# One-hot tiles in pairs of tokens, and a longer first part of the expert layer, in a hybrid decoder layer

## The chip, the cores and the metric

The kernel runs on one core of one Trainium2 chip. The metric is the device time of one execution in microseconds (us); of several executions the median is taken. A profile is one execution recorded by the hardware profiler; its span is the time from its first to its last recorded instruction. The engines are TensorE (PE for its matmuls, PEld for its weight loads), VectorE (DVE), ScalarE (ACT), GpSimd (POOL) and SyncE (SP), which issues most DMAs.

## The reference

One decoder layer over 256 tokens of width 1024: a convolution branch and a sparse attention branch, a cross attention over 256 memory rows, and then a mixer that chooses among 16,384 experts. The change lies in that mixer alone:

```python
q = (hn @ w_q).reshape(B, T, PEER_HEADS, 2, PEER_HALF)
s = jnp.einsum('bthpd,hpkd->bthpk', q, sub_keys).astype(jnp.float32)
s_top, i_top = lax.top_k(s, PEER_TOPK)
cand = s_top[..., 0, :, None] + s_top[..., 1, None, :]
cand_idx = i_top[..., 0, :, None] * PEER_KEYS + i_top[..., 1, None, :]
best, pos = lax.top_k(cand.reshape(B, T, PEER_HEADS, n_cand), PEER_TOPK)
experts = jnp.take_along_axis(cand_idx.reshape(B, T, PEER_HEADS, n_cand), pos, axis=-1)
gates = jax.nn.softmax(best, axis=-1)
...
a = jax.nn.gelu(jnp.einsum('nd,nkd->nk', xc, u))
return jnp.einsum('nk,nkd->nd', gc * a, v_emb[ec])
```

Each token has 8 heads with 16 experts each. An expert's number is a pair (i1, i2) of two numbers below 128.

## The kernel before

**The expert mixer as dense products.** The kernel gathers no expert rows. It computes gelu(u . x) for all 16,384 experts and all tokens, multiplies by a matrix of gates that is zero where an expert was not chosen, and multiplies the result with all rows of v. The experts come in 128 chunks of 128 (KEYS = 128). Chunk i holds, with i2 fixed to i, the 128 values of i1 on the partitions, and a tile of 256 tokens beside them.

**A chunk of u (`u_chunk`, L989).** One DMA on SP brings 512 KB (`raw`, four buffers). `wsplit` makes of each half a rounded part `hi` on ACT (L137) and a remainder `lo` (L138) on an engine that the call names: GpSimd (G) for chunks below J = 36, VectorE (V) for the others. `proj` then runs 24 matmuls of 256 columns (L148 to L150: hi x hn_h, hi x hn_l, lo x hn_h for eight slices of the width). A gelu on ACT empties the PSUM tile `pu`.

**The choice.** Meanwhile VectorE finds for each half (hf) of the tokens the top 16 of each of the 16 score rows, builds the sums, takes their top 16 (L901 to L926), subtracts the best (`ge`, L928), and works out the chosen pairs (L931 to L953) as two tables `ix`. `choice_gates` (L959) then takes the exponential of `ge` on ACT (L962), sums and divides on VectorE (L964 to L967). `picked_out` (L970) turns i1, i2 and the gate of a half by a transpose on PE and stores them as f16 tiles i1T, i2T, gTh and gTl (128 choices on the partitions, 256 tokens).

**The first part (loop at L994).** For chunks 0 to J-1 the gelu (L999) goes to `slA`. `choice_gates` is written before chunk J-12 = 24, the six calls of `picked_out` before chunks J-6 to J-1.

**The second part (`while`, L1025).** Chunks J to 127 go on, and the gate matrix is built four tokens at a time in 64 blocks (`gates4`, L1004), spread evenly over chunks. A block makes four one-hot tiles of 128 x 4 numbers on VectorE: o1 (128 choices against the 128 values of i1, L1011), o2 (against i2, L1012), and o2 times the two parts of the gate, oh and ol (L1013, L1014). The token is the innermost of a tile's two axes. For each of the four tokens two matmuls of 128 columns follow (L1016 with oh, L1017 with ol), with o1[:, :, j] as weights and oh[:, :, j] as moving operand, so 128 x 128 gates per token in the PSUM tile `pw`. VectorE multiplies the part of `pw` whose chunks are done into slA and slB (L1021); ACT copies the rest into slB (L1022), where the gelu of a later chunk is multiplied in (L1030, L1034).

**The value part (loop at L1074).** For each chunk, 12 matmuls of 512 columns add the gated activations times v into four PSUM tiles Y (L1070). `gfin`, the gain of the final norm, is written in the text with value chunk 122 (L1081) and takes the place of `hn_l`, which the last chunk of u reads.

**The order of the work.** PE runs in the order of the text. The instructions of the other engines are ordered when the program is built, by a planner with its own estimates of durations; each engine then runs its queue strictly in that order. Buffers of one tag (o0 to o3, `hi`, `lo`, `raw`, `pw`) are reused in turn, and an instruction that overwrites one waits for its readers.

Of the kernel before, what the change touches and what calls it, by code (L numbers as in the profile page):

```python
# [12 lines left out]
F16 = mybir.dt.float16  # L13
# [3 lines left out]
ALU = mybir.AluOpType  # L17
# [3 lines left out]
P = 128  # L21
# [71 lines left out]
def build(tc, A, out, dbg=None):  # L93
    nc = tc.nc
    V, S, G, PE = nc.vector, nc.scalar, nc.gpsimd, nc.tensor
# [13 lines left out]
    def C(name):  # L109
        a, b = CC[name]  # L110
        return con1[:, a:b] if b <= NCON1 else con2[:, a - NCON1:b - NCON1]
# [8 lines left out]
    def wload(src, n=1024):  # L120
        cnt[0] += 1
        raw = wts.tile([P, 1024], F32, name=f"raw{cnt[0]}", tag="raw", bufs=4)
        if cnt[0] == 1:
            nc.sync.dma_start(raw[:, 0:512], src[:, 0:512])
            nc.sync.dma_start(raw[:, 512:], src[:, 512:])
        else:
            nc.sync.dma_start(raw[:, 0:n], src)
        return raw, cnt[0]

    def wsplit(w, engs=None, width=P, half=512):  # L130
        raw, i = w
        out_ = []
        for q in range(2):
            hi = wts.tile([P, 512], F32R, name=f"hi{i}{q}", tag="hi", bufs=6)[:, 0:half]
            lo = wts.tile([P, 512], F32R, name=f"lo{i}{q}", tag="lo", bufs=6)[:, 0:half]
            r = raw[:, half * q:half * q + half]
            S.activation(hi, r, AF.Copy)  # L137
            (engs or (V, V))[q].tensor_sub(lo, r, hi.bitcast(F32))  # L138
            for j in range(half // width):
                out_.append((hi[:, j * width:(j + 1) * width], lo[:, j * width:(j + 1) * width]))  # L140
        return out_

    def wchunk(src, engs=None, width=P):

        return wsplit(wload(src), engs, width)

    def mm3(ps, w, xh, xl, start, stop):
        PE.matmul(ps, w[0], xh, start=start, stop=False)  # L148
        PE.matmul(ps, w[0], xl, start=False, stop=False)  # L149
        PE.matmul(ps, w[1], xh, start=False, stop=stop)  # L150

    def proj(ps, w, x, ks=range(KC)):
        for k in ks:
            mm3(ps, w[k], x[0][:, k], x[1][:, k], k == 0, k == KC - 1)
# [7 lines left out]
    i1T, i2T, gTh, gTl = [tk.tile([P, T], F16, name=n) for n in ("i1T", "i2T", "gTh", "gTl")]  # L162
# [12 lines left out]
    def psum(w, name, tag="mm"):  # L175
        return pm.tile([P, 512], F32, name=name, tag=tag, bufs=4)[:, :w]
# [82 lines left out]
    u = ch.tile([P, 4, 30 + T], F32, name="u")  # L259
# [84 lines left out]
    for i in range(2):  # L344
        G.memset(KV[i], 0.0)
        ps = psum(T, f"pkv{i}")
# [44 lines left out]
    for i in range(6):  # L391
        dst = kraw[i] if i < 2 else qraw[:, i - 2]
        ps = psum(T, f"pq{i}")
# [83 lines left out]
    for i in range(2):  # L477
# [3 lines left out]
        for jj in range(16):  # L481
            PE.matmul(phv, w1[i][:, jj], KV[i][:, :, 2 * jj:2 * jj + 16 * (NC_CMP - 1) + 1:16],
                      start=(jj == 0), stop=(jj == 15))
# [216 lines left out]
    for i in range(2, KC):  # L700
        ps = psum(T, f"pwo{i}")
# [118 lines left out]
    for i in range(2, KC):  # L820
        ps = psum(T, f"pmw{i}")
# [27 lines left out]
    for i in range(16):  # L849
        ps = psum(T, f"ppq{i}")  # L850
# [16 lines left out]
    hn_h = h2p.tile([P, KC, T], F32R, name="hn_h", tag="act_h")  # L867
    hn_l = h2p.tile([P, KC, T], F32R, name="hn_l", tag="act_l")
# [13 lines left out]
    for nh, c in ((0, 0), (1, 0), (1, 1), (0, 1)):  # L882
        PE.matmul(Y[nh][c], zero[:, 0:P], zero, start=True, stop=False, skip_group_check=True)
        for k in range(4):
            PE.matmul(Y[nh][c][:, k * P:(k + 1) * P], h2T[:, 4 * c + k, nh * P:(nh + 1) * P], C("ident"),
                      start=False, stop=False, skip_group_check=True)
# [9 lines left out]
    for hf in range(2):  # L896
# [36 lines left out]
        for side in range(2):  # L933
# [12 lines left out]
            oh = tp.tile([P, 16, P], F16, name=f"ohx{hf}{side}", tag="ohx")  # L946
# [12 lines left out]
    def choice_gates():  # L959
        for hf in range(2):  # L960
            ge = picked[hf][2]
            S.activation(ge, ge, AF.Exp)  # L962
            gs = tp.tile([P, 8], F32, name=f"gs{hf}", tag="gs")
            V.tensor_reduce(gs, ge, axis=AX.X, op=ALU.add)  # L964
            V.reciprocal(gs, gs)
            gt = picked[hf][2] = tp.tile([P, P], F32, name=f"gt{hf}", tag=f"gt{hf}")
            V.tensor_tensor(gt.rearrange("p (k h) -> p h k", h=8), ge, gs.unsqueeze(2).to_broadcast([P, 8, 16]), op=ALU.mult)  # L967
            show(f"g_{hf}", gt)

    def picked_out(hf, j):  # L970

        sl = slice(hf * P, hf * P + P)
        pt = pp.tile([P, 512], F32, name=f"ptk{hf}{j}", tag="w", bufs=2)[:, 0:P]
        PE.transpose(pt, picked[hf][j], C("ident"))
        if j < 2:
            S.activation((i1T, i2T)[j][:, sl], pt, AF.Copy)
        else:
            S.activation(gTh[:, sl], pt, AF.Copy, scale=GSC)
            V.scalar_tensor_tensor(gTl[:, sl], pt, GSC, gTh[:, sl], op0=ALU.mult, op1=ALU.subtract)


    J = 36
    e1 = outer.enter_context(tc.tile_pool(name="e1", bufs=1, side="left", **RW))
    slA = e1.tile([P, J, T], F32, name="slA")
    tmp = outer.enter_context(tc.tile_pool(name="tmp", bufs=2, side="left", **RW))
    iota4 = tmp.tile([P, P, 4], F16, name="iota4", bufs=1)
    V.tensor_copy(iota4, C("iota").unsqueeze(2).to_broadcast([P, P, 4]))

    def u_chunk(i):  # L989
        ps = pp.tile([P, 512], F32, name=f"pu{i}", tag="w" if i < J - 8 and i % 4 > 1 else "s", bufs=2)[:, 0:T]  # L990
        proj(ps, wchunk(A["u"][i], (G, G) if i < J else (V, V)), (hn_h, hn_l))
        return ps

    for i in range(J):  # L994
        if i == J - 12:
            choice_gates()
        if i >= J - 6:
            picked_out((i - J + 6) // 3, (i - J) % 3)
        S.activation(slA[:, i], u_chunk(i), AF.Gelu_apprx_tanh)  # L999
# [3 lines left out]

    def gates4(n0, done):  # L1004
        pw = pp.tile([P, 512], F32, name=f"pw{n0}", tag="w", bufs=2).rearrange("p (n i) -> p n i", n=4)
        o1, o2, oh, ol = [tmp.tile([P, P, 4], F16, name=f"o{t}{n0}", tag=f"o{t}", bufs=1 if t == 1 else 2) for t in range(4)]

        def over_i(t):
            return t[:, n0:n0 + 4].unsqueeze(1).to_broadcast([P, P, 4])

        V.tensor_tensor(o1, iota4, over_i(i1T), op=ALU.is_equal)  # L1011
        V.tensor_tensor(o2, iota4, over_i(i2T), op=ALU.is_equal)  # L1012
        V.tensor_tensor(oh, o2, over_i(gTh), op=ALU.mult)  # L1013
        V.tensor_tensor(ol, o2, over_i(gTl), op=ALU.mult)  # L1014
        for j in range(4):
            PE.matmul(pw[:, j], o1[:, :, j], oh[:, :, j], start=True, stop=False)  # L1016
            PE.matmul(pw[:, j], o1[:, :, j], ol[:, :, j], start=False, stop=True)  # L1017
        for sl_, x0, x1 in ((slA, 0, J), (slB, J, done)):
            if x1 > x0:
                va = sl_[:, 0:x1 - x0, n0:n0 + 4].rearrange("p i n -> p n i")  # L1020
                V.scalar_tensor_tensor(va, pw[:, :, x0:x1], 1.0 / GSC, va, op0=ALU.mult, op1=ALU.mult)  # L1021
        S.activation(slB[:, done - J:, n0:n0 + 4].rearrange("p i n -> p n i"), pw[:, :, done:], AF.Copy, scale=1.0 / GSC)  # L1022

    i, ng = J, 0
    while i < KEYS or ng < T:  # L1025
        if i < KEYS:
            ps = u_chunk(i)
            if ng:
                tt = tmp.tile([P, T], F32, name=f"ua{i}", tag="ua", bufs=3)
                S.activation(tt[:, 0:ng], ps[:, 0:ng], AF.Gelu_apprx_tanh)  # L1030
            if ng < T:
                S.activation(slB[:, i - J, ng:], ps[:, ng:], AF.Gelu_apprx_tanh)
            if ng:
                V.tensor_mul(slB[:, i - J, 0:ng], slB[:, i - J, 0:ng], tt[:, 0:ng])  # L1034
            i += 1
        while ng < min(T, (i - J) * T // (KEYS - 3 - J)):
            gates4(ng, i)
            ng += 4
# [35 lines left out]
    for i in range(KEYS):  # L1074
        a = slA[:, i] if i < J else slB[:, i - J]
# [94 lines left out]
```

## Time and profile before

| | |
|---|---|
| median of 3 runs (lowest, highest) | 1144.11 us (1143.82, 1146.87) |
| the profiled execution, its own time | 1143.92 us |
| its span | 1142.1 us |
| mean granted TensorE clock, share of full | 0.984 |
| PE busy / PEld busy | 1095.2 us (96%) / 1005.4 us (88%) |
| DVE busy / ACT busy / POOL busy | 884.2 us (77%) / 591.8 us (52%) / 111.2 us (10%) |

Busy time is the union of an engine's recorded instructions. An instruction's duration overlaps the next one's on the same engine, so what an instruction costs in a row of others is the distance from its start to the next start. Matmuls overlap most; their ends are modelled, their starts are recorded. In the timeline a row gives start, duration, engine, line, operation, tile written <- tiles read, and in brackets the idle time ahead of it and what ended it.

The mixer's stages in the span: the first part up to about 463 us, the second up to about 785 us, the value part to the end.

### The profile page before, as it was taken

What the parts mean: (1) busy time and instruction counts of PE and PEld (TensorE: products, weight loads), DVE (VectorE), ACT (ScalarE), POOL (GpSimd) and SP (SyncE); (2) the same over time, 40 slices, a digit from 0 to 9 for tenths busy, and PEclk for the clock granted to TensorE, in tenths of its full rate; (3) what the DMA queues carried; (4) which work ended last, traced back from release to release, by engine and by line L of the source; (5) the groups of instructions that cost most, each with busy time, mean ns of one, the idle gap of its engine ahead of it and who ended that gap; (6) DMA issues with size and microseconds to landing.
All of it is one profiled execution on the core that took longest, in us unless ns stands there. A gap on an engine that the chain in (4) does not pass through costs nothing.

```text
span 1142.1 us, 20622 instructions
## 1 busy us (share of the span) xinstructions
PE 1095.2 (96%) x7361; PEld 1005.4 (88%) x7362; DVE 884.2 (77%) x2229; ACT 591.8 (52%) x1354; POOL 111.2 (10%) x86
## 2 busy tenths in 40 slices
PE   8889999999999489999999999999999999999997
PEld 7878778999999489999999999999888888888885
DVE  7998847888889994778888889996666666666665
ACT  5731456665455155555555554445555555555554
POOL 0000000000068389000000000000000000000000
PEclk9899999999999889999999999999999999999999
DMA  8542224625434235544444454446555566565662
GB/s 277 194 127 94 74 99 152 197 90 185 154 124 149 93 114 200 167 156 141 150 147 160 137 161 137 151 144 203 191 196 193 194 192 195 192 196 191 196 192 86
DMA packets 51688, 182.47 MB, mean 160 GB/s; under 512 B 5761, under 2 KB 6529, under 8 KB 51457
## 3 DMA queue, kind: packets, MB, share of 16 engines
q1 hardware_dynamic: 51296, 180.62, 48.2%
q8 instruction: 58, 0.95, 0.3%
q10 hardware_dynamic: 288, 0.52, 0.1%
q14 instruction: 46, 0.37, 0.1%
HBM read 179.81 MB, written 1.05 MB: 158 GB/s over the span
## 4 chain that ended last, share of the span: by engine, by line
PE 87%; DVE 4%; issue 3%; POOL 2%; DMA 1%; ACT 1%; SPq 0%; POOLq 0%; ACTq 0%; DVEq 0%
PE Y L1070 30%; PE pu L150 10%; PE pu L149 10%; PE pu L148 10%; PE pw L1016 3%; PE pw L1017 3%; PE pmk L442 3%; POOL lo L138 2%; PE pmv L458 2%; PE ppq L148 1%; PE ppq L149 1%; PE ppq L150 1%; DVE lo L138 1%; PE pmw L149 1%; PE pmw L148 1%
## 5 line engine op out<-in xcount | busy, mean ns | idle before, releaser
L137 ACT ACTIVATE hi<-raw 128x512 fp32r<-128x512 f32 x632 | 380.6, 624 | 198.7 <-PE pu L149 78.0
L138 DVE TENSOR_TENSOR lo<-raw,hi 128x512 fp32r<-128x512 f32 (+1 forms) x560 | 371.1, 685 | 32.8 <-ACT hi L137 26.4
L148 PE MATMUL pu<-hn_h,hi 128*128 128x256 f32 x1024 | 296.9, 290 | 18.3 <-ACT hi L137 18.3
L150 PE MATMUL pu<-hn_h,lo 128*128 128x256 f32 x1024 | 291.6, 285 | 2.5 <-POOL lo L138 2.5
L149 PE MATMUL pu<-hn_l,hi 128*128 128x256 f32 x1024 | 290.8, 284 | 0.0
L148 PEld LDWEIGHTS pu<-hn_h,hi 128*128 128x128 f32 x1024 | 198.0, 193 | 18.7 <-ACT hi L137 18.5
L150 PEld LDWEIGHTS pu<-hn_h,lo 128*128 128x128 f32 x1024 | 196.7, 192 | 4.6 <-POOL lo L138 4.5
L149 PEld LDWEIGHTS pu<-hn_l,hi 128*128 128x128 f32 x1024 | 197.2, 193 | 0.0
L1070 PE MATMUL Y<-hi,ah 128*128 128x512 f32 x512 | 158.2, 389 | 0.0
L1070 PE MATMUL Y<-lo,ah 128*128 128x512 f32 x512 | 158.1, 389 | 0.0
L1070 PE MATMUL Y<-hi,al 128*128 128x512 f32 x512 | 158.1, 389 | 0.0
L1070 PEld LDWEIGHTS Y<-lo,ah 128*128 128x128 f32 x512 | 96.1, 188 | 20.0
L1070 PEld LDWEIGHTS Y<-hi,al 128*128 128x128 f32 x512 | 96.1, 188 | 19.8
L1070 PEld LDWEIGHTS Y<-hi,ah 128*128 128x128 f32 x512 | 96.1, 188 | 19.9
L158 DVE TENSOR_TENSOR al<-slB,ah 128x256 fp32r<-128x256 f32 x92 | 39.1, 425 | 89.9 <-PE Y L1070 89.9
L138 POOL TENSOR_TENSOR lo<-raw,hi 128x512 fp32r<-128x512 f32 x72 | 103.7, 1473 | 36.6 <-ACT hi L137 36.3
L157 ACT ACTIVATE ah<-slB 128x256 fp32r<-128x256 f32 x92 | 38.5, 418 | 115.7 <-PE Y L1070 115.7
L1022 ACT ACTIVATE slB<-pw 128x364 f32<-128x364 f32 (+31 forms) x64 | 33.3, 521 | 67.3 <-DVE slB L1021 50.1
L1017 PE MATMUL pw<-o,o 128*128 128x128 f16 x256 | 64.2, 297 | 0.0
L1016 PE MATMUL pw<-o,o 128*128 128x128 f16 x256 | 63.6, 294 | 0.0
L273 DVE SCALAR_TENSOR_TENSOR yc<-u,par,yc 128x256 f32<-128x256 f32 x120 | 55.9, 477 | 0.3
L1013 DVE TENSOR_TENSOR o<-o,gTh 128x512 f16<-128x512 f16 x64 | 28.5, 445 | 30.9 <-PE pw L1016 30.5
(387 smaller groups left out, 1754.1 us busy)
## 6 DMA issues: line engine op xcount, KB each, us to landing
raw<-u SPq DMA_DIRECT2D x128, 512.0 KB, 3.3
raw<-v SPq DMA_DIRECT2D x128, 512.0 KB, 4.3
raw<-peer_w_q SPq DMA_DIRECT2D x16, 512.0 KB, 3.3
raw<-w_in_t SPq DMA_DIRECT2D x15, 512.0 KB, 6.0
raw<-w_mem_k SPq DMA_DIRECT2D x8, 512.0 KB, 3.4
raw<-w_mem_v SPq DMA_DIRECT2D x8, 512.0 KB, 3.4
raw<-w_out SPq DMA_DIRECT2D x8, 512.0 KB, 3.9
raw<-w_mem_q SPq DMA_DIRECT2D x8, 512.0 KB, 3.3
```

The costliest lines, as they stand in the source:

```text
L137: S.activation(hi, r, AF.Copy)
L138: (engs or (V, V))[q].tensor_sub(lo, r, hi.bitcast(F32))
L148: PE.matmul(ps, w[0], xh, start=start, stop=False)
L149: PE.matmul(ps, w[0], xl, start=False, stop=False)
L150: PE.matmul(ps, w[1], xh, start=False, stop=stop)
L157: S.activation(dst[0], src, AF.Copy)
L158: V.tensor_sub(dst[1], src, dst[0].bitcast(F32))
L273: V.scalar_tensor_tensor(yc[:, i], u[:, i, j:j + T], w, yc[:, i], op0=ALU.mult, op1=ALU.add)
L442: PE.matmul(ps, wr[:, k * P:(k + 1) * P], mg[:, k], start=(k == 0), stop=(k == KC - 1))
L1016: PE.matmul(pw[:, j], o1[:, :, j], oh[:, :, j], start=True, stop=False)
L1017: PE.matmul(pw[:, j], o1[:, :, j], ol[:, :, j], start=False, stop=True)
L1070: PE.matmul(Y[nh][c], lhs[:, sl], wc[c][t], start=False, stop=i == KEYS - 1 and lhs is a[1], skip_group_check=True)
```

## The change

The one-hot tiles keep their 512 numbers per partition, but the four tokens of a block are laid out as two pairs: the axes are pair, value, token within the pair. The matmuls read a token of a pair, o1[:, q, :, r], with a step of two numbers instead of four. The repeated table `iota4` (128 x 4) becomes `iota2` (128 x 2), read for both pairs. J becomes 44, so that slA holds 44 chunks and slB 84; `choice_gates` is written before chunk J-8 = 36, `picked_out` before chunks 38 to 43. GpSimd makes `lo` for chunks below 32, VectorE from there on. The PSUM tag "w" serves two of every four chunks of u up to chunk J-9 = 35, where it went up to 27.

```diff
--- before.py
+++ after.py
@@ -979,20 +979,20 @@
             V.scalar_tensor_tensor(gTl[:, sl], pt, GSC, gTh[:, sl], op0=ALU.mult, op1=ALU.subtract)
 
 
-    J = 36
+    J = 44
     e1 = outer.enter_context(tc.tile_pool(name="e1", bufs=1, side="left", **RW))
     slA = e1.tile([P, J, T], F32, name="slA")
     tmp = outer.enter_context(tc.tile_pool(name="tmp", bufs=2, side="left", **RW))
-    iota4 = tmp.tile([P, P, 4], F16, name="iota4", bufs=1)
-    V.tensor_copy(iota4, C("iota").unsqueeze(2).to_broadcast([P, P, 4]))
+    iota2 = tmp.tile([P, P, 2], F16, name="iota2", bufs=1)
+    V.tensor_copy(iota2, C("iota").unsqueeze(2).to_broadcast([P, P, 2]))
 
     def u_chunk(i):
         ps = pp.tile([P, 512], F32, name=f"pu{i}", tag="w" if i < J - 8 and i % 4 > 1 else "s", bufs=2)[:, 0:T]
-        proj(ps, wchunk(A["u"][i], (G, G) if i < J else (V, V)), (hn_h, hn_l))
+        proj(ps, wchunk(A["u"][i], (G, G) if i < 32 else (V, V)), (hn_h, hn_l))
         return ps
 
     for i in range(J):
-        if i == J - 12:
+        if i == J - 8:
             choice_gates()
         if i >= J - 6:
             picked_out((i - J + 6) // 3, (i - J) % 3)
@@ -1003,18 +1003,20 @@
 
     def gates4(n0, done):
         pw = pp.tile([P, 512], F32, name=f"pw{n0}", tag="w", bufs=2).rearrange("p (n i) -> p n i", n=4)
-        o1, o2, oh, ol = [tmp.tile([P, P, 4], F16, name=f"o{t}{n0}", tag=f"o{t}", bufs=1 if t == 1 else 2) for t in range(4)]
+        o1, o2, oh, ol = [tmp.tile([P, 2, P, 2], F16, name=f"o{t}{n0}", tag=f"o{t}", bufs=1 if t == 1 else 2) for t in range(4)]
 
         def over_i(t):
-            return t[:, n0:n0 + 4].unsqueeze(1).to_broadcast([P, P, 4])
-
-        V.tensor_tensor(o1, iota4, over_i(i1T), op=ALU.is_equal)
-        V.tensor_tensor(o2, iota4, over_i(i2T), op=ALU.is_equal)
+            return t[:, n0:n0 + 4].rearrange("p (a b) -> p a b", b=2).unsqueeze(2).to_broadcast([P, 2, P, 2])
+
+        i4 = iota2.unsqueeze(1).to_broadcast([P, 2, P, 2])
+        V.tensor_tensor(o1, i4, over_i(i1T), op=ALU.is_equal)
+        V.tensor_tensor(o2, i4, over_i(i2T), op=ALU.is_equal)
         V.tensor_tensor(oh, o2, over_i(gTh), op=ALU.mult)
         V.tensor_tensor(ol, o2, over_i(gTl), op=ALU.mult)
         for j in range(4):
-            PE.matmul(pw[:, j], o1[:, :, j], oh[:, :, j], start=True, stop=False)
-            PE.matmul(pw[:, j], o1[:, :, j], ol[:, :, j], start=False, stop=True)
+            q, r = j // 2, j % 2
+            PE.matmul(pw[:, j], o1[:, q, :, r], oh[:, q, :, r], start=True, stop=False)
+            PE.matmul(pw[:, j], o1[:, q, :, r], ol[:, q, :, r], start=False, stop=True)
         for sl_, x0, x1 in ((slA, 0, J), (slB, J, done)):
             if x1 > x0:
                 va = sl_[:, 0:x1 - x0, n0:n0 + 4].rearrange("p i n -> p n i")
```

## Rows read from the trace of the kernel before

**Rows 1.** The page, part 4: the chain that ended last, by line.

```profile
PE Y L1070 30%; PE pu L150 10%; PE pu L149 10%; PE pu L148 10%; PE pw L1016 3%; PE pw L1017 3%; PE pmk L442 3%; POOL lo L138 2%; PE pmv L458 2%; PE ppq L148 1%; PE ppq L149 1%; PE ppq L150 1%; DVE lo L138 1%; PE pmw L149 1%; PE pmw L148 1%
```

**Rows 2.** Windows of core 0: stretch, its us, busy us of each engine, clock.

```profile
380.00:400.00 20.00, 5.06 (x43) 4.85 (x41) 20.00 (x139) 0.00 (x0) 2.52 (x3) 0.74 0.17 55
...
460.00:500.00 40.00, 40.00 (x337) 39.56 (x336) 29.35 (x74) 22.63 (x53) 0.00 (x0) 1.00 0.51 163
...
620.00:660.00 40.00, 40.00 (x337) 39.52 (x336) 35.14 (x84) 20.34 (x54) 0.00 (x0) 1.00 0.46 151
...
740.00:776.00 36.00, 36.00 (x304) 35.56 (x303) 33.04 (x71) 16.97 (x48) 0.00 (x0) 1.00 0.45 152
```

**Rows 3.** Timeline, PE: start, us, engine, line; first gate block, then the last.

```profile
463.57 0.29 PE L1016 MATMUL pw<-o,o 128*128 128x128 f16 x1
...
773.62 0.28 PE L1016 MATMUL pw<-o,o 128*128 128x128 f16 x1
```

**Rows 4.** Timeline, PE, around one gate block of the middle.

```profile
602.09 0.28 PE L149 MATMUL pu<-hn_l,hi 128*128 128x256 f32 x1
602.21 0.28 PE L150 MATMUL pu<-hn_h,lo 128*128 128x256 f32 x1
...
603.03 0.30 PE L1016 MATMUL pw<-o,o 128*128 128x128 f16 x1
603.15 0.29 PE L1017 MATMUL pw<-o,o 128*128 128x128 f16 x1
...
603.40 0.28 PE L149 MATMUL pu<-hn_l,hi 128*128 128x256 f32 x1
```

**Rows 5.** Source lines L560 and L1016: durations in ns, min/median/max.

```profile
L560 PE MATMUL pss<-causb,identb x32: 219/224/230, 104.1 to 171.9; 128*128 128x128 bf16 x32
...
L1016 PE MATMUL pw<-o,o x256: 285/296/301, 463.6 to 774.3; 128*128 128x128 f16 x128
```

**Rows 6.** Timeline around one pair of L560.

```profile
104.09 0.28 PE L560 MATMUL pss<-causb,identb 128*128 128x128 bf16 x2
104.21 0.43 PE L442 MATMUL pmk<-mg,raw 128*128 128x256 f32 x1
```

**Rows 7.** Timeline, DVE, one gate block late in the second loop.

```profile
745.81 0.42 DVE L1012 TENSOR_TENSOR o<-iota,i2T 128x512 f16<-128x512 f16 x1
746.14 0.47 DVE L1021 SCALAR_TENSOR_TENSOR slA<-pw,slA 128x144 f32<-128x144 f32 x1
746.53 0.38 DVE L1034 TENSOR_TENSOR slB<-slB,ua 128x228 f32<-128x228 f32 x1
746.83 0.88 DVE L1021 SCALAR_TENSOR_TENSOR slB<-pw,slB 128x320 f32<-128x320 f32 x1
747.63 0.67 DVE L138 TENSOR_TENSOR lo<-raw,hi 128x512 fp32r<-128x512 f32 x1
748.23 0.41 DVE L1011 TENSOR_TENSOR o<-iota,i1T 128x512 f16<-128x512 f16 x1
```

**Rows 8.** Timeline, DVE: L916 and the instruction behind it.

```profile
392.10 0.58 DVE L916 TENSOR_TENSOR cd<-top 128x416 f32<-128x416 f32 x1
392.59 0.09 DVE L906 MATCH_VALUE_LOAD tix<-top,s 128x8 f32 x1
```

**Rows 9.** Timeline, ACT: the two exponentials and what stands about them.

```profile
376.94 0.36 ACT L999 ACTIVATE slA<-pu 128x256 f32<-128x256 f32 x1
...
402.51 0.31 ACT L962 ACTIVATE ge<-ge 128x128 f32<-128x128 f32 x1 [23.91 <-DVE ge L928]
...
410.85 0.37 ACT L999 ACTIVATE slA<-pu 128x256 f32<-128x256 f32 x1
...
461.37 0.37 ACT L999 ACTIVATE slA<-pu 128x256 f32<-128x256 f32 x1
```

**Rows 10.** Tile gfin: first and last start last, as in rows 5.

```profile
L1081 SPq DMA_DIRECT2D gfin<-fin_g x1: 327/327/327, 786.1 to 786.1; - x1
```

**Rows 11.** Timeline, DVE, after the selection.

```profile
444.01 1.30 DVE L1011 TENSOR_TENSOR o<-iota,i1T 128x512 f16<-128x512 f16 x1 [12.65 <-ACT i1T L976]
```

## The prediction

> **What bounds the kernel now.** I read the chain of waits by line first. The reader is to see that TensorE owns it: the second product over the values (Y) has 30%, the first product over the keys' experts (pu, three lines) 30%, and the one-hot products pw (L1016, L1017) 6% [rows 1]. So an edit pays in full only where TensorE never waits. The windows say where that is: from 460 us to the end of the second loop PE is busy all of the time at full clock, while from 380 to 400 us it has 5.06 of 20 us, the clock is down to 0.74, ACT does nothing and DVE is full [rows 2]. The change touches both places. Third, the timelines of PE, DVE and ACT for the price of one gate block and for what holds the stall.
>
> There are 64 gate blocks. From the first matmul of the first to that of the last are 310.05 us over 63 intervals, 4.92 us each [rows 3]. In that time the loop does 89/64 = 1.39 chunks of 24 matmuls at 0.12 us (2.88 us a chunk) and one block of eight pw matmuls [rows 4].
>
> **One-hot tiles in pairs: TensorE.** A pw matmul streams 128 columns of 2-byte numbers, and follows the one before by 0.12 us (0.117 over the eight) [rows 4]. L560 also streams 128 columns of 2-byte numbers, but densely: two of them and the start of the next line take 104.09 to 104.21, 0.06 each, and one lasts 224 ns where pw lasts 296 [rows 6, 5]. What differs is the step between columns: 2 bytes there, four tokens (8 bytes) in pw. pu reads columns 4 bytes apart (they are 4-byte numbers) at 0.12 us for 256, again 0.06 for 128 [rows 4]. After the change pw's step is two tokens, 4 bytes. No row has 2-byte numbers at that step; the ends are 0.117 (no gain) and 0.06 (the dense price). I take 0.06, since both the 2-byte and the 4-byte pitch run at it and only the 8-byte pitch does not. From the pu matmul ahead of a block to the second one behind it are 1.19 us, 0.95 more than two plain steps; the last pw and the turn back to pu hold 0.25 of that [rows 4]. I leave the turn as it is and count seven steps: 7 x 0.057 = 0.40 us a block, 64 x 0.40 = 25.6 us. If the last step and the turn shrink too it is 30 us.
>
> **The same tiles: VectorE.** The four one-hot operations keep 512 elements each; only the operand that is repeated now has rows of two numbers, not four. One costs 0.33 us from its start to the next (745.81 to 746.14) [rows 7]. At half the rate it would cost what L138 costs, 0.60 for 512 four-byte elements; below, nothing excludes a few hundredths less, but the 512 results stay. The nearest row is L916: there one 4-byte word is read again and again beside a dense operand, and 416 elements take 0.49 us, 1.18 ns each, the same as L138's 0.60/512 = 1.17 [rows 8, 7]. A pair of 2-byte numbers is also one 4-byte word read again and again. I take 0.33, no change.
>
> **What is late next.** VectorE. Per block it now does four one-hots (1.32), the two products into slA and slB (0.39 + 0.80 late on) and, per chunk, two lo (0.60 each) and one multiplication (0.30): 1.32 + 1.19 + 1.39 x 1.50 = 4.60 us of 4.92 at the end [rows 7]. The windows agree: busy 29.35 of 40 us at first, 35.14 in the middle, 33.04 of 36 at the end, so 3.61, 4.32 and 4.52 us a block [rows 2]. It grows because slB's product covers more rows with each chunk done.
>
> **44 chunks in the first part.** The second loop has 84 chunks, and 81/64 = 1.27 to a block. TensorE: 0.125 x 2.88 = 0.36 us less a block, but the eight chunks (23 us) are done in the first part instead, so this alone gives nothing. A block then costs 4.92 - 0.36 - 0.40 = 4.16 on TensorE. VectorE loses 0.125 x 1.50 = 0.19 a block late, 0.16 early; slB's product starts with eight more rows done, 32 elements at (0.88 - 0.47)/(320 - 144) = 2.3 ns, so 0.07 more at first and none at the end. It needs 3.52 early, 4.18 in the middle, 4.33 to 4.41 late. So TensorE sets the pace of the first half and VectorE of the second: the excess grows from none to about 0.25 over 32 blocks, 4 us. In-order queues that wait on each other seldom reach their full share; VectorE idles 2.96 of 36 us late on now [rows 2]. If that 8% stays when it is the bound, it is 32 x 4.3 x 0.08 = 11 us more; if none stays, nothing. I take 5.
>
> The lo of chunks 32 to 35 go from POOL to VectorE: 8 x 0.60 = 4.8 us where VectorE idles 12.65 us in one piece [rows 11]; without that cover it would lengthen the selection by as much. No DMA is added, and the u loads on SP keep their order. iota2 is half of iota4, done once, off the path. The gates' transposes come with chunks 38 to 43, still ahead of the first block. slA's product grows by what slB's loses.
>
> **The exponentials.** The stall at 380 us is the second exponential (L962): ACT stands at it for 23.91 us, until DVE's L928 has given its operand at 402 us, and behind it stand the hi copies that every later chunk needs [rows 9]. Counting L999, the gelu before it is chunk 14, and chunk 18 comes at 410.85: 33.9 us for four chunks that are worth 11.5, so 22.4 us lost. But the code has both exponentials at chunk 24. They were moved ahead of their place in the text, as soon as the plan thought their operand ready. How far such a move goes is shown by gfin: written with value chunk 122, its load is issued at 786.1, when the value loop has just begun [rows 10]. Writing the exponentials at chunk 36 instead of 24 changes nothing that the plan weighs at chunk 14. I take: the stall stays, 0; the other end is 22 us.
>
> **Sum.** 25.6 - 4 - 5 = 16.6 us. The profiled execution took 1143.92 us (span 1142.1 and 1.8 around it), 0.2 under the median; 1143.9 - 16.6 = 1127.3, so 1127.
>
> **Rivals.** (a) The exponentials do wait until chunk 36, about 441 us at 2.9 us a chunk, when L928 is done. The stall goes: 1127 - 22 = 1105. For: the text says so. Against: rows 9 and 10.
> (b) The change doesn't do what it says: pw's pace is not set by the step, or any step but the dense one costs double. Then TensorE keeps 0.95 a block and the time stays at 1144, 3 us either way. Against: the 72 ns between L560 and pw [rows 5]. [...] The trace does not agree that the 8-byte step is free: 0.117 against 0.06.
> (c) Slower: the one-hot operations get dearer for their rows of two, in the second loop, where VectorE is already the bound. Its mean of 4.02 us a block stands against 4.92 - 0.36 = 4.56 for a draw, so it decides from 0.54 a block, 0.135 an operation. At 0.60 each it is 64 x (4.02 + 1.08 - 4.56) = 35 us, 1179; just past the draw, 1147. Against: L916's price. [...]
>
> **Chances.** Forecast 0.63 (1116 to 1137, between all 30 us kept and 11 lost to VectorE on top of 4), (a) 0.18, (b) 0.11, (c) 0.08. The range leaves out most of (c), the low side of (a) and part of (b): 1099 to 1143. A measurement of this kernel tells about 0.3%, 3.4 us, from no change. Faster: the forecast, (a) and a little of (b), 0.83; same: most of (b) and the draw of (c), 0.10; slower 0.07.
>
> **What would show it.** pw matmuls 0.06 apart and near 224 ns; one-hot operations still 0.33 apart; blocks 4.2 us apart early and longer late, DVE above 97% there and PE waiting for its one-hots or lo; ACT's gap of some 24 us still before chunk 15. The prediction is wrong if pw stays at 0.117, if ACT has no gap, or if a one-hot takes over 0.4.

## The result, and the profile after

The changed kernel takes 1119.11 us (median of 4 runs, 1118.01 to 1120.72) against 1145.49 us (4 runs, 1143.82 to 1147.61) for the kernel before beside it: ratio 0.9777, interval 0.9761 to 0.9792, so 26.4 us less. The forecast was 1127. The profiled execution took 1120.72 us, its span is 1118.9 us, 23.2 less than the span before.

Line numbers have moved by one or two: o1 to ol are L1012 to L1015, pw L1018 and L1019, the products L1023, the copy by ACT L1024, Y L1072.

First the windows of the changed kernel (columns as in [rows 2]).

```profile
380.00:400.00 20.00, 7.62 (x64) 7.42 (x62) 20.00 (x137) 1.17 (x1) 5.08 (x5) 0.75 0.26 85
...
460.00:500.00 40.00, 40.00 (x348) 39.87 (x347) 27.15 (x57) 23.10 (x53) 0.00 (x0) 1.00 0.54 173
500.00:540.00 40.00, 40.00 (x373) 39.57 (x372) 35.49 (x93) 24.18 (x60) 0.00 (x0) 1.00 0.49 159
540.00:580.00 40.00, 40.00 (x369) 39.61 (x368) 37.33 (x96) 23.56 (x59) 0.00 (x0) 1.00 0.50 162
580.00:620.00 40.00, 40.00 (x372) 39.57 (x372) 37.49 (x94) 21.79 (x57) 0.00 (x0) 1.00 0.49 161
620.00:660.00 40.00, 40.00 (x368) 39.61 (x368) 39.59 (x95) 22.00 (x59) 0.00 (x0) 1.00 0.50 162
660.00:700.00 40.00, 40.00 (x373) 39.53 (x372) 39.89 (x93) 20.11 (x56) 0.00 (x0) 1.00 0.49 154
700.00:740.00 40.00, 39.77 (x369) 39.20 (x367) 40.00 (x91) 18.68 (x57) 0.00 (x0) 1.00 0.47 150
740.00:760.00 20.00, 19.39 (x168) 18.89 (x169) 19.82 (x42) 10.52 (x32) 0.00 (x0) 1.00 0.59 183
```

Two things are to be seen. The stall at 380 us is still there. In the second loop VectorE fills up to 40.00 of 40 us, and yet TensorE idles only 0.23 us of the stretch from 700 to 740 and 0.61 of the next.

Next the timeline of PE around a gate block (answers to [rows 4]), then the durations of pw ([rows 5]).

```profile
600.89 0.28 PE L150 MATMUL pu<-hn_h,lo 128*128 128x256 f32 x1
601.02 0.23 PE L1018 MATMUL pw<-o,o 128*128 128x128 f16 x1
601.09 0.22 PE L1019 MATMUL pw<-o,o 128*128 128x128 f16 x1
601.14 0.22 PE L1018 MATMUL pw<-o,o 128*128 128x128 f16 x1
...
601.66 0.28 PE L149 MATMUL pu<-hn_l,hi 128*128 128x256 f32 x1
```

```profile
L1018 PE MATMUL pw<-o,o x256: 218/218/231, 489.1 to 753.7; 128*128 128x128 f16 x128
L1019 PE MATMUL pw<-o,o x256: 218/218/220, 489.1 to 753.8; 128*128 128x128 f16 x128
```

A pw matmul lasts 218 ns instead of 296 and follows the one before by 0.057 us. From the pu matmul ahead of a block to the second one behind it are 0.77 us instead of 1.19: 0.42 less a block.

The first and the last block (answers to [rows 3]), and VectorE's last block of one-hots with what follows (answers to [rows 7]).

```profile
489.06 0.23 PE L1018 MATMUL pw<-o,o 128*128 128x128 f16 x1
...
753.37 0.23 PE L1018 MATMUL pw<-o,o 128*128 128x128 f16 x1
```

```profile
749.16 0.41 DVE L1012 TENSOR_TENSOR o<-iota,i1T 128x512 f16<-128x512 f16 x1
749.49 0.41 DVE L1014 TENSOR_TENSOR o<-o,gTh 128x512 f16<-128x512 f16 x1
749.83 0.41 DVE L1015 TENSOR_TENSOR o<-o,gTl 128x512 f16<-128x512 f16 x1
750.16 1.28 DVE L138 TENSOR_TENSOR lo<-raw,hi 128x512 fp32r<-128x512 f32 x2
...
756.26 0.55 DVE L1023 SCALAR_TENSOR_TENSOR slA<-pw,slA 128x176 f32<-128x176 f32 x1
```

The one-hots stand 0.33 to 0.34 us apart, as before. The second loop's 63 intervals take 264.31 us instead of 310.05.

Last the exponential on ACT (answers to [rows 9]) and VectorE behind the selection (answers to [rows 11]).

```profile
379.50 0.36 ACT L999 ACTIVATE slA<-pu 128x256 f32<-128x256 f32 x1
379.88 1.28 ACT L962 ACT_TABLE_LOAD   x1
404.95 0.31 ACT L962 ACTIVATE ge<-ge 128x128 f32<-128x128 f32 x1 [23.78 <-DVE ge L928]
```

```profile
444.57 0.96 DVE L138 TENSOR_TENSOR lo<-raw,hi 128x512 fp32r<-128x512 f32 x1 [10.77 <-ACT hi L137]
```

ACT waits 23.78 us at L962 where it waited 23.91. Written twelve chunks later, the exponential sits as early in ACT's queue as before. VectorE idles 10.77 us ahead of chunk 32's `lo`, so taking these over from GpSimd was covered.

### The profile page after: what moved, and what is told of

The parts are those of the page before. It is cut to its first block, busy times and chain, and to the rows that moved or that the text cites. A ratio compares the mean times of both kernels' runs of the same rounds, so it can differ in the third digit from the quotient of the medians.

```text
span 1118.9 us, 20590 instructions
## 1 busy us (share of the span) xinstructions
PE 1069.8 (96%) x7362; PEld 980.4 (88%) x7362; DVE 881.4 (79%) x2229; ACT 585.0 (52%) x1347; POOL 100.8 (9%) x78
## 5 line engine op out<-in xcount | busy, mean ns | idle before, releaser
L138 DVE TENSOR_TENSOR lo<-raw,hi 128x512 fp32r<-128x512 f32 (+1 forms) x568 | 377.6, 686 | 49.5 <-ACT hi L137 44.2
L1072 PE MATMUL Y<-hi,ah 128*128 128x512 f32 x512 | 158.2, 389 | 0.0
L1072 PE MATMUL Y<-hi,al 128*128 128x512 f32 x512 | 158.1, 389 | 0.0
L1072 PE MATMUL Y<-lo,ah 128*128 128x512 f32 x512 | 158.1, 389 | 0.0
L1072 PEld LDWEIGHTS Y<-lo,ah 128*128 128x128 f32 x512 | 96.1, 188 | 20.0
L1072 PEld LDWEIGHTS Y<-hi,al 128*128 128x128 f32 x512 | 96.1, 188 | 19.9
L1072 PEld LDWEIGHTS Y<-hi,ah 128*128 128x128 f32 x512 | 96.0, 188 | 19.9
L158 DVE TENSOR_TENSOR al<-slB,ah 128x256 fp32r<-128x256 f32 x84 | 35.7, 425 | 82.2 <-PE Y L1072 82.2
L138 POOL TENSOR_TENSOR lo<-raw,hi 128x512 fp32r<-128x512 f32 x64 | 93.3, 1493 | 36.5 <-ACT hi L137 36.2
L157 ACT ACTIVATE ah<-slB 128x256 fp32r<-128x256 f32 x84 | 35.1, 418 | 105.6 <-PE Y L1072 105.6
L1024 ACT ACTIVATE slB<-pw 128x332 f32<-128x332 f32 (+31 forms) x64 | 31.5, 492 | 83.3 <-DVE slB L1023 69.4
L158 DVE TENSOR_TENSOR al<-slA,ah 128x256 fp32r<-128x256 f32 x44 | 19.2, 437 | 40.8 <-PE Y L1072 40.8
L157 ACT ACTIVATE ah<-slA 128x256 fp32r<-128x256 f32 x44 | 18.4, 418 | 54.4 <-PE Y L1072 53.0
L148 PE MATMUL ppq<-gx_h,hi 128*128 128x256 f32 x128 | 37.3, 292 | 0.0
```

The lines of the kernel that those rows point to most:

```text
L157: S.activation(dst[0], src, AF.Copy)
L158: V.tensor_sub(dst[1], src, dst[0].bitcast(F32))
L1072: PE.matmul(Y[nh][c], lhs[:, sl], wc[c][t], start=False, stop=i == KEYS - 1 and lhs is a[1], skip_group_check=True)
```

## The experiments

Two questions were put. What made the 26 us: the matmuls' step alone, or the longer first part too; and if the step, which operand's. And why VectorE, full for 100 us, cost next to nothing. The exponentials, which did not move, were tried by themselves.

**The pairs alone.** J and all places that hang on it as before; only the tiles in pairs.

```diff
-    J = 44
+    J = 36
-        ... (G, G) if i < 32 else (V, V)
+        ... (G, G) if i < J else (V, V)
-        if i == J - 8:
+        if i == J - 12:
```

> The one-hot tiles in pairs, with the first part as before (36 chunks, POOL for their lo, exponentials written at chunk 24). Theory T1 (the whole gain is TensorE's 0.41 us in each of the 64 blocks; the longer first part only takes load off VectorE, whose lag the buffers cover anyway): blocks of 4.905 - 0.41 = 4.50 us, about 1119 us, ratio to before 0.975 to 0.980. Rival T2 (the longer first part carries part of the gain, since VectorE needs 4.5 us and more per block in the last third and would hold TensorE there): TensorE waits for one-hots or lo late in the second loop, blocks of 4.6 to 4.7 us there, 1124 to 1132 us, ratio 0.983 to 0.990.

Measured: 1118.47 us (5 runs), ratio 0.9765 (0.9751 to 0.9778), the same as the whole change within its interval. The chain of waits by line of this kernel answers to [rows 1]; pw went from 3% and 3% to 1% and 1%. (In the changed kernel the chain can be followed back to 740 us only.)

```profile
PE Y L1072 31%; PE pu L148 10%; PE pu L150 10%; PE pu L149 10%; PE pmk L442 3%; POOL lo L138 2%; PE pmv L458 2%; PE pw L1018 1%; PE ppq L148 1%; PE ppq L149 1%; PE ppq L150 1%; PE pw L1019 1%; DVE lo L138 1%; PE pmw L149 1%; PE pmw L148 1%
```

Over eight blocks with eleven chunks of u among them, blocks stand 4.48 us apart where they stood 4.905: 0.42 x 64 = 27 us, and the span is 1114.7 us, 27.4 less than before. So the pairs hold all of the gain.

**The 44 chunks alone.** Tiles in fours as before, everything else as changed.

```diff
-        o1, o2, oh, ol = [tmp.tile([P, 2, P, 2], F16, ...
+        o1, o2, oh, ol = [tmp.tile([P, P, 4], F16, ...
-            PE.matmul(pw[:, j], o1[:, q, :, r], oh[:, q, :, r], start=True, stop=False)
+            PE.matmul(pw[:, j], o1[:, :, j], oh[:, :, j], start=True, stop=False)
```

> The 44 chunks, the lo of chunks 32 on by VectorE and the exponentials written at chunk 36, with the one-hot tiles in fours as before. T1: nothing of it lies on TensorE's path and the exponentials stand where they stood on ACT, so 1145 us, ratio 0.997 to 1.003, and ACT's gap of 24 us stays. T2: 1130 to 1140 us, with a shorter gap or with less waiting in the second loop.

Measured: 1144.71 us (10 runs), ratio 0.9993 (0.9984 to 1.0003). The last exponential ran at 403.4 us. The longer first part and the new place of the exponentials are worth nothing by themselves.

**The exponentials held back.** The changed kernel, with the gates' softmax ordered behind the gelu of the chunk ahead of its place in the text.

```diff
-            choice_gates()
+            with tc.issue_after(gelu.ins):
+                choice_gates()
...
-        S.activation(slA[:, i], u_chunk(i), AF.Gelu_apprx_tanh)
+        gelu = S.activation(slA[:, i], u_chunk(i), AF.Gelu_apprx_tanh)
```

> The changed kernel, with an edge that keeps both exponentials behind the gelu of chunk 35 on ACT, which is what the text alone was to do. T1 (the stall is only ACT's queue standing at an exponential whose operand VectorE delivers at about 405 us): no gap on ACT there, PE busy through 380 to 420, 22 us less than the changed kernel, about 1097 us. Rival T3 (VectorE's chain is the true bound: beside POOL's lo it ends much later, and the gates' transposes at chunk 38 wait for it): the stall moves behind chunk 36 and less than 10 us are won, 1109 us or more.

Measured: 1100.26 us (4 runs), ratio 0.96 (0.9585 to 0.9614): 18.9 us under the changed kernel. Its windows where the stall was, and its waits from 420 to 440 us (engine, line, what it waited for: us in total, times, longest):

```profile
380.00:400.00 20.00, 20.00 (x169) 20.00 (x168) 20.00 (x111) 10.60 (x22) 19.88 (x16) 1.00 0.63 210
...
420.00:440.00 20.00, 16.30 (x116) 16.10 (x116) 14.54 (x26) 7.39 (x15) 0.00 (x0) 0.83 0.39 132
```

```profile
PE pu L150 <- DVE lo L138: 3.7, 1, 3.7
```

PE is busy all through the old stall. What stays is a wait of 3.7 us for chunk 32's `lo`, the first that VectorE makes: it stands behind the selection in VectorE's queue. So the cover of [rows 11] goes as soon as TensorE stops waiting. The selection itself also ends later. L928, of the changed kernel and then of this one:

```profile
L928 DVE TENSOR_TENSOR ge<-best x2: 258/259/260, 350.4 to 404.7; 128x128 f32<-128x128 f32 x2
```

```profile
L928 DVE TENSOR_TENSOR ge<-best x2: 611/795/979, 349.3 to 410.8; 128x128 f32<-128x128 f32 x2
```

**Held, and GpSimd up to chunk 35.**

```diff
-        ... (G, G) if i < 32 else (V, V)
+        ... (G, G) if i < 36 else (V, V)
```

> The kernel with the exponentials held behind chunk 35, and POOL making the lo up to chunk 35 instead of 31. There TensorE lost 3.7 us at chunk 32, and ran at half clock behind that, because VectorE's first lo stood behind the rest of the selection until 427 us. Theory T1: with POOL on these chunks the wait is gone, 3 to 5 us less, 1095 to 1097 us. Rival T3: POOL's lo slow VectorE's chain down as much, the exponentials' sums and the transposes at chunk 38 come late, and the time stays at 1100 us or more.

Measured: 1094.48 us (4 runs), ratio 0.9559 (0.9543 to 0.9576). PE is busy 19.44 of 20 us from 420 to 440. It is the fastest version, 24.6 us under the changed kernel and 5.8 under the held one, a little more than the 3 to 5 that were expected.

**Held, with the old first part.** Pairs, J = 36, the softmax held to chunk 30.

```diff
-        if i == J - 12:
-            choice_gates()
+        if i == J - 6:
+            with tc.issue_after(gelu.ins):
+                choice_gates()
```

> Pairs, 36 chunks in the first part with POOL's lo for all of them, and the exponentials held behind chunk 29, just ahead of the first transpose: what the hold is worth without the longer first part. Theory T1 (the longer first part is worth nothing of its own): within 4 us of the held kernel with 44 chunks, 1096 to 1104 us. Rival T4 (with the stall gone the selection on VectorE needs the longer first part, for its tables come at 430 us and more): TensorE waits at the transposes of chunks 32 to 35 for 5 us or more, 1105 us and up.

Measured: 1102.95 us (4 runs), ratio 0.9627 (0.9611 to 0.9643). The gates' transpose on PE and a window of this kernel:

```profile
432.51 0.45 PE L974 MATMUL ptk<-con,gt 128*128 128x128 f32 x1 [9.20 <-DVE gt L967]
```

```profile
420.00:440.00 20.00, 10.80 (x71) 10.63 (x71) 18.01 (x31) 6.82 (x16) 8.66 (x7) 0.74 0.25 79
```

Now it is TensorE's queue that stands still: the transpose comes with chunk 32, 9.20 us before its gates are ready, and the granted clock falls to 0.74. Against the version before it the longer first part is worth 8.5 us. (The two also differ in the chunk behind which the exponentials are held, 29 here and 35 there: with the shorter first part the transposes come with chunks 30 to 35 already.) It had no value only while the exponential's stall delayed everything.

**Weights in fours, moving operand in pairs.** o1 in the old layout (8 bytes from column to column), o2, oh and ol in pairs.

```diff
-            PE.matmul(pw[:, j], o1[:, q, :, r], oh[:, q, :, r], start=True, stop=False)
+            PE.matmul(pw[:, j], o1[:, :, j], oh[:, q, :, r], start=True, stop=False)
```

> The changed kernel with o1 alone back in fours, so the weights of pw are read 8 bytes apart and the moving operands 4 bytes apart. Theory M (the moving operand's step sets pw's pace): pw still 0.057 us apart, 1119 us. Rival W (the weights' step sets it): pw 0.117 apart, blocks 0.41 us longer, about 1145 us.

Measured: 1119.04 us (one run). The first and the last block of this kernel:

```profile
485.81 0.25 PE L1023 MATMUL pw<-o,o 128*128 128x128 f16 x1
...
751.63 0.25 PE L1023 MATMUL pw<-o,o 128*128 128x128 f16 x1
```

The second loop takes 265.82 us where the changed kernel takes 264.31. So the step of the weights costs 1.5 us at most, which doesn't show in the total.

**Moving operand in fours, weights in pairs.** The reverse.

```diff
-            PE.matmul(pw[:, j], o1[:, q, :, r], oh[:, q, :, r], start=True, stop=False)
+            PE.matmul(pw[:, j], o1[:, q, :, r], oh[:, :, j], start=True, stop=False)
```

> The changed kernel with o2, oh and ol back in fours and o1 in pairs: the counterpart of the run with the weights in fours. Theory M (only the moving operand's step sets pw's pace): pw 0.117 us apart again, the blocks 0.41 us longer, about 1145 us. If pw stays at 0.057, no single operand sets it and the pace comes only with both in fours.

Measured: 1143.35 us (one run). All of the gain is gone. pw of this kernel:

```profile
L1023 PE MATMUL pw<-o,o x256: 278/296/300, 486.9 to 776.6; 128*128 128x128 f16 x128
```

Over eight blocks with ten chunks of u among them, blocks stand 4.53 us apart, 0.41 more than the 4.12 of the changed kernel.

**One operand at 16 bytes.** As the last, but oh spread so that its columns stand 16 bytes apart; ol stays at 8.

```diff
-        o1, o2, oh, ol = [tmp.tile([P, P, 4] if t > 0 else ...
+        o1, o2, oh, ol = [tmp.tile([P, P, 8] if t == 2 else [P, P, 4] if t else ...
-        V.tensor_tensor(oh, o2, over_4(gTh), op=ALU.mult)
+        V.tensor_tensor(oh[:, :, 0:4], o2, over_4(gTh), op=ALU.mult)
```

> As the run with the moving operands in fours, but oh stands in a tile of eight numbers per value of which four are used: the pw matmuls with oh read 16 bytes apart, those with ol 8 bytes apart. If the pace goes with the bytes stepped over, the oh matmuls take 0.23 us and a block 0.47 us more than there (5.00 us, some 1173 us); if there is one price for every step that is too wide, they take 0.117 and the time stays near 1143 us.

Measured: 1172.26 us (one run), blocks 4.97 us apart by the same reckoning. Timeline of PE, one with oh and one with ol and the next two:

```profile
602.91 0.41 PE L1023 MATMUL pw<-o,o 128*128 128x128 f16 x1
603.14 0.30 PE L1024 MATMUL pw<-o,o 128*128 128x128 f16 x1
603.25 0.41 PE L1023 MATMUL pw<-o,o 128*128 128x128 f16 x1
603.48 0.30 PE L1024 MATMUL pw<-o,o 128*128 128x128 f16 x1
```

The 16-byte step takes 0.23 us for 128 columns, the 8-byte step beside it 0.11 to 0.12.

**All dense.** The token outermost: no step at all in the matmuls, and in the one-hots one number repeated 128 times.

```diff
-        o1, o2, oh, ol = [tmp.tile([P, 2, P, 2], F16, ...
+        o1, o2, oh, ol = [tmp.tile([P, 4, P], F16, ...
-            return t[:, n0:n0 + 4].rearrange("p (a b) -> p a b", b=2).unsqueeze(2).to_broadcast([P, 2, P, 2])
+            return t[:, n0:n0 + 4].unsqueeze(2).to_broadcast([P, 4, P])
```

> The changed kernel with the token as the outermost axis of the one-hot tiles: all pw operands dense (2 bytes apart), and on VectorE one 2-byte number repeated 128 times as the second operand. Theory M: pw gains nothing more (0.057 us apart as with pairs). For VectorE two prices: 0.33 us an operation as with pairs, then 1119 us; or one element at a time as with 4-byte numbers, 0.60 us, then a block needs 1.08 us more on VectorE, 4.8 us early and 5.4 late against 4.2, some 1165 to 1175 us, and PE waits for VectorE throughout.

Measured: 1166.82 us (one run). pw lasts 219 ns, 0.055 us apart where the pairs have 0.057: next to nothing more to win on TensorE below 4 bytes. VectorE of this kernel, and a window late in the second loop:

```profile
600.75 0.71 DVE L1012 TENSOR_TENSOR o<-iota,i1T 128x512 f16<-128x512 f16 x1
601.35 0.72 DVE L1013 TENSOR_TENSOR o<-iota,i2T 128x512 f16<-128x512 f16 x1
601.95 0.71 DVE L138 TENSOR_TENSOR lo<-raw,hi 128x512 fp32r<-128x512 f32 x1
```

```profile
700.00:740.00 40.00, 32.53 (x285) 30.58 (x285) 40.00 (x74) 16.43 (x46) 0.00 (x0) 1.00 0.37 119
```

A one-hot now costs 0.60 us, 0.27 more: 64 x 4 x 0.27 = 69 us of work on an engine that was nearly full, and the kernel is 48 us slower than the changed one.

**One more one-hot.** The changed kernel with a fifth operation of the same kind in each block, whose result nobody reads.

```diff
+        ox = tmp.tile([P, 2, P, 2], F16, name=f"ox{n0}", tag="ox", bufs=1)
+        V.tensor_tensor(ox, o2, over_i(gTh), op=ALU.mult)
```

> The changed kernel with a fifth one-hot operation in each block, whose result nobody reads: 0.33 us more on VectorE, 64 times, 21 us in all. From the windows VectorE needs 3.7 us a block early and 4.3 late against TensorE's 4.20; with 0.33 more it needs 4.05 to 4.63. Theory L (VectorE's excess is taken out of the lead that the one-hots have over pw and out of the products' lag behind it, some 5 us together): the excess of 12 us comes out as 5 to 7 us, 1124 to 1126 us. The forecast's reckoning (every us over TensorE's pace is lost, and some for the queues): 12 us or more, 1131 us and up. If VectorE were no bound at all: 1119 us.

Measured: 1126.95 us (4 runs), ratio 0.9841 (0.9825 to 0.9858), 7.8 us over the changed kernel for 64 x 0.33 = 21 us of work. That is just above the 5 to 7 us of theory L and well under the 12 of the forecast's reckoning. Windows of this kernel:

```profile
460.00:500.00 40.00, 40.00 (x351) 39.83 (x350) 29.57 (x67) 22.82 (x52) 0.00 (x0) 1.00 0.49 163
...
580.00:620.00 40.00, 40.00 (x372) 39.57 (x371) 39.93 (x102) 21.74 (x58) 0.00 (x0) 1.00 0.48 161
...
660.00:700.00 40.00, 38.71 (x352) 37.35 (x351) 40.00 (x96) 17.52 (x53) 0.00 (x0) 1.00 0.44 145
700.00:740.00 40.00, 37.84 (x328) 35.71 (x328) 40.00 (x92) 17.39 (x54) 0.00 (x0) 1.00 0.43 143
```

From 460 to 700 us VectorE idles 12.4 us here and 23.1 in the changed kernel (the sum of what its busy time leaves of each window). So 10.7 of the 21 us went into idle time, 7.8 into the end, and the other 2 to 3 into the lateness that is described below.

## Why the prediction held, and which term was off

**pw's step: right, mechanism and size.** 0.40 us a block was forecast, 0.42 came; 64 x 0.42 = 27 us, where the sum had 25.6. That it is the moving operand's step, which the prediction took for granted, is shown by the two mixed layouts: 1119.04 with only the weights stepping over 8 bytes, 1143.35 with only the moving operand doing so. Rival (b) is out with it: with the moving operand at an 8-byte step a matmul of 128 columns takes 0.117 us, at 4 bytes 0.057.

**The one-hots on VectorE: right.** 0.33 was forecast, 0.33 to 0.34 came. Rival (c) is out for pairs. A single repeated number, however, costs 0.60 for 512 in the dense layout (600.75 to 601.35), the half rate named as the upper end.

**VectorE as what is late next: the term that was off.** The prediction charged 4 us for its excess over TensorE and 5 for queues that wait on each other. Measured are 0.23 + 0.61 = 0.8 us of PE's busy time. By the starts of the blocks it is 1.15: early on an interval with one chunk of u takes 3.40 us and one with two 6.28, so the 46 and 17 of them would take 263.16 us, where 264.31 were measured. That VectorE would be full was right (40.00 of 40). The step that failed is turning each late microsecond into one at the end.

VectorE may run late for a while before TensorE feels it. One-hots are made ahead of their matmuls: counting blocks, L1015 of the eighth starts 7.0 us before its pw (below), that of the last 3.5 (749.83 to 753.37). And the product into slA may follow its pw late: 0.95 us behind the first (490.01 to 489.06), 4.94 behind the last but one (746.75 to 751.69), 2.89 behind the last (753.37 to 756.26).

```profile
511.58 0.42 DVE L1015 TENSOR_TENSOR o<-o,gTl 128x512 f16<-128x512 f16 x1
```

```profile
518.62 0.23 PE L1018 MATMUL pw<-o,o 128*128 128x128 f16 x1
```

One-hots and products stand in the one queue of VectorE, so this is one lateness seen at two places and must not be added up: some 3.5 us. With the 1.15 us that TensorE lost it comes near the 4 us of excess in the sum. So the size of the excess was about right, and most of it was absorbed. The 5 us for waiting queues did not come: VectorE idled 0.00 and 0.18 us in the last two windows, not 8%, so this queue, though it waits on others, did come to its full share.

Where TensorE did wait, it was not for one-hots or `lo`, as the prediction expected, but for a pu tile that ACT had not emptied:

```profile
738.74 0.24 ACT L1024 ACTIVATE slB<-pw 128x36 f32<-128x36 f32 x1 [2.73 <-DVE slB L1023]
...
740.15 0.17 ACT L1034 ACTIVATE slB<-pu 128x16 f32<-128x16 f32 x1
```

```profile
740.38 0.39 PE L148 MATMUL pu<-hn_h,hi 128*128 128x256 f32 x1 [0.61 <-ACT slB L1034]
```

ACT's copy of pw waits for VectorE's late product into slB, and the gelu that empties pu stands behind that copy in ACT's queue. With a fifth one-hot PE's windows fall short by 1.29 and 2.16 us from 660 on, mostly by the same route. Waits of that kernel from 460 to 762 us (us in total, times, longest; L1026 is the copy, L1036 the gelu):

```profile
ACT slB L1026 <- DVE slB L1025: 98.0, 53, 4.0
```

```profile
PE pu L148 <- ACT slB L1036: 3.4, 8, 0.8
...
PE pw L1020 <- DVE o L1014: 0.2, 1, 0.2
```

The lead of its one-hots runs out too: it is 0.1 us in five of the last nine blocks. That lead and lag absorb VectorE's excess is argued from starts, from waits and from the one-hot added; a run with fewer buffers was not made.

**44 chunks, `lo` from GpSimd to VectorE: right.** Nothing by themselves (0.9993). The cover was VectorE's idle time, 10.77 us after; without it the price is seen in the held version, where PE waits 3.7 us, and 5.8 us between the two held versions.

**The exponentials: right that the stall stays.** ACT's gap is 23.78 us. Of rival (a) the price was right and the condition wrong: the stall goes for 18.9 us, or 24.6 with GpSimd's `lo`, against the 22 named, but not by moving the call in the text. It takes an order between instructions.

**The sum.** 27 - 1 + 0 = 26 against 26.4 measured by the medians. The spans show 23.2 because that one execution was 2.6 us late from early on: its first matmul of L442 starts at 86.79 us against 84.22 before, far ahead of all that was changed, and the first exponential at 350.7 against 348.1. 2.6 + 23.2 = 25.8. The forecast of 1127 was 8 us high, nearly all of it the 9 us charged for VectorE; the time lies inside the forecast's range because its low end let VectorE cost nothing.

## What to carry to other kernels

Lay out a matmul's moving operand of 2-byte numbers so that its columns stand 4 bytes apart (128 columns took 0.057 us, against 0.117 at 8 bytes), and let VectorE repeat a pair of 2-byte numbers, not a single one (512 results took 0.33 us, against 0.60); the pair does both at once. Before charging time for an engine that becomes full, measure how late it may run before its partner waits, and look for that wait also by way of a third engine; charge only the excess beyond it (here 21 us of added work cost 7.8). Where an engine stalls on an instruction that stands too early in its queue, moving the line in the program may change nothing if a planner orders the queue (ACT's wait was 23.91 us and stayed 23.78): hold it behind a named instruction (18.9 us less), and then look again at the parts that were worth nothing while the stall hid them.

## What the runs showed of the hardware that was not expected

- The price of the moving operand's step grew with the bytes from 4 to 16: 128 columns of 2-byte numbers took 0.055 us dense, 0.057 at 4 bytes, 0.117 at 8 and 0.23 at 16. With the weights at a step of 8 bytes the 64 blocks take 1.5 us more, and the total is the same.
- A VectorE operation on 128 x 128 four-byte numbers (L928) lasts 259 ns where GpSimd's work had run out, and 611 and 979 ns in the held version, where GpSimd is at work beside it. The held selection ends 6.1 us later (410.8 against 404.7). The changed kernel shows the like within one run: an operation on 128 x 128 four-byte numbers lasts 0.21 us at 404.98 (L936) and 1.27 at 405.99 (L940), just after GpSimd has resumed at 405.86. Not every operation is slowed: in the changed kernel L964, which reads 128 x 128 such numbers, lasts 0.26 us at 404.23, with GpSimd idle, and 0.27 at 420.92, with GpSimd busy. That GpSimd is the cause was not tried by itself.
